# A two-block transformer on one core: GpSimd's elementwise work moved to VectorE, and the gate, up and MLP products turned feature-major

## The chip, the cores and the metric

The kernel runs on one core of a Trainium2 chip. TensorE multiplies, VectorE (DVE), ScalarE (ACT) and GpSimd (POOL) work element by element, SyncE (SP) issues the transfers of the weights. The metric is the time of one execution on the device in microseconds (us); less is better.

## The reference

The input is one sequence of 256 tokens with 1024 features, all in float32. Block 1 has two layers; a layer adds to the residual x a SwiGLU feed-forward (FFN), a mixer and a second FFN. Cut to the parts that the change touches:

```python
def ffn(x, w):                       # D = 1024, F = 2816
    h = rmsnorm(x) * w.norm
    x = x + 0.5 * (silu(h @ w.gate) * (h @ w.up)) @ w.down

def mixer(x, w):                     # one input projection w_in, one output projection w_out
    h = rmsnorm(x) * w.norm_mix
    # three branches: gated linear attention with per-channel decay (hg),
    # gated delta rule with short convolutions (q, k, v), gated linear recurrence (rg)
    x = x + concat(hg, delta, rg) @ w.out

def mlp(x, w):                       # in block 2
    h = rmsnorm(x) * w.g_pre_mlp
    x = x + rmsnorm(relu(h @ w.up) ** 2 @ w.down) * w.g_post_mlp     # 1024 -> 4096 -> 1024
```

Block 2 has one layer: retention and dilated attention with a gated sum (combine), the MLP above, and a gate with an additional input (PLE). All weight matrices are read once, 290 MB in all.

## The kernel before

Every weight comes in chunks of two 128-row tiles by 512 columns ([128, 2, 512], 512 KB), in the order of use, loaded by SP's queue into one of four `raw` buffers. A product is made in float32r, a reduced float32, and is exact by parts: the weight w is split into wh (rounded) and wl = w - wh, the operand x into xh and xl, and three products are accumulated: xh·wh, xh·wl, xl·wh. In `wchunk` ScalarE casts wh (line 94) and another engine subtracts wl: GpSimd (line 97) or VectorE (line 99). Which one, the text in `split_on` says, one letter a chunk in turn: "ppv" in the FFNs and in block 2, so two of three on GpSimd. In the mixer the letters stand behind each step's name in `MIX_ORDER`. There are three buffers each for wh and wl, so ScalarE's cast of a chunk waits until TensorE is through with the one three before.

There are two forms of product. `gemm_tok` (through `mm_tok`, lines 146 to 148) is token-major: the stationary operand is a tile of 128 tokens, the moving one 512 weight columns, the result [token, column]. `gemm_feat` (lines 190 to 192) is feature-major: the stationary operand is a tile of 128 weight columns, the moving one all 256 tokens, the result [column, token]. Both take the same chunks.

`ffn` goes over the hidden columns in groups of 512 (the last has 256). Gate g and up u come token-major; per tile of 128 tokens ScalarE makes tanh(r g / 2), where r is the norm's factor of a token, and VectorE (1 + tanh)·g (line 319) and the product with u and r²/2 (line 320). The down product needs the hidden values with columns on partitions, so `hidden_T` transposes them on TensorE, 128x128 at a time (line 295, tile htr), and `split` casts the high part (ScalarE, line 199) and subtracts the low part (VectorE, line 200). `mlp` does the same with a squared relu in place of the gate. `norm_T` transposes x, weights and splits it (ScalarE line 202, VectorE line 203; tiles xTh, xTl) and makes r; with `by_tok` it takes the first 128 tokens first (transposes of line 262), without it pairs of both token tiles (line 275).

The mixer's steps are written out in `MIX_ORDER`; besides remainders GpSimd takes some of its elementwise work: masks of the triangular solve (lines 718, 719), parts of the halving levels of the hg scores (lines 871, 900, 901, 903, by the letters of `HG_POOL`), and four operations of the recurrence (lines 988, 989, 995, 996). `r_broadcast` (lines 471, 472) puts r on all partitions along the token axis, by products with a matrix of ones; the mixer and block 2's entry use it. The framework's scheduler decides in which order the instructions of each engine are issued, from the order of the program and the free buffers; each engine then runs its own in that order.

Of the kernel before, what the change touches and what calls it, by code (L numbers as in the profile page):

```python
# [231 lines left out]
class Stream:  # L232
    """The residual stream, token-major, and its transposed and weighted form for the next product."""
# [67 lines left out]

def ffn(c, st, wT, wg, wu, wd, F):
    nc = c.nc
    xs, r = st.norm_T(wT)
    rh = c.small.tile([P, 2], F32, tag="rh", name=c.nm("rh"))
    rr = c.small.tile([P, 2], F32, tag="rr", name=c.nm("rr"))
    nc.vector.tensor_scalar(rh, r, 0.5, None, op0=ALU.mult)
    nc.vector.tensor_tensor(rr, rh, r, op=ALU.mult)
# [1204 lines left out]
```

## Time and profile before

| | before |
|---|---|
| median of 3 runs | 1861.69 us (1858.45 to 1861.82) |
| profiled execution, span from first to last instruction | 1858.6 us |
| TensorE (PE) busy | 1764.4 us, 95%, 9216 products |
| TensorE's weight loads (PEld) busy | 1488.6 us, 80% |
| VectorE (DVE) busy | 935.6 us, 50% |
| ScalarE (ACT) busy | 896.4 us, 48% |
| GpSimd (POOL) busy | 925.1 us, 50% |
| mean granted clock of TensorE | 0.974 |
| read from memory | 289.47 MB, 156 GB/s over the span |

The lowest of the runs (1858.45 us) is within 0.2 us of the span of the profiled execution, so little lies around the span. A busy share is a mean over the whole program: the FFNs, the mixers and block 2 differ. Products overlap, so the busy time of one is longer than the distance to the next; for what a product costs, the distance between starts is to be read.

### The profile page before, as it was taken

To read this page: it belongs to the slowest core of one execution; us is meant where nothing else is said; L and a number is where in the kernel's file an instruction comes from. 1 tells how busy PE (TensorE), PEld (TensorE's weight loads), DVE (VectorE), ACT (ScalarE), POOL (GpSimd) and SP (SyncE) were. 2 spreads that over 40 slices of the span, in tenths; PEclk is the share of its full clock that TensorE was granted. 3 is DMA by queue.
4 is the path that set the end of the run, shared out by engine and by line. 5 is a ranking of instruction groups with operands and counts; after the bars stand their busy time and mean duration, and the time that the engine had idled before them with its cause. 6 is when DMAs were issued, how large, how long until landed. Compare 5 with 4: busy or idle time off the path is not lost.

```text
span 1858.6 us, 24550 instructions
## 1 busy us (share of the span) xinstructions
PE 1764.4 (95%) x9216; PEld 1488.6 (80%) x9216; DVE 935.6 (50%) x1744; ACT 896.4 (48%) x1364; POOL 925.1 (50%) x449
## 2 busy tenths in 40 slices
PE   8999988999999999987889999999999999999995
PEld 6888877978888788877878888788878888778884
DVE  5334599853333332299964333533556543643246
ACT  4445563444444444455345445455444544555453
POOL 4556455235555555544415556454433455555561
PEclk9999988899999999998989999999999999999998
DMA  6546432235555555532224545455333456545561
GB/s 221 181 159 206 162 111 74 87 102 181 182 193 182 181 182 181 182 137 91 69 100 169 177 163 205 153 184 173 127 134 114 158 176 209 181 164 181 182 227 45
DMA packets 91639, 292.13 MB, mean 157 GB/s; under 512 B 11008, under 2 KB 23808, under 8 KB 91520
## 3 DMA queue, kind: packets, MB, share of 16 engines
q1 hardware_dynamic: 91376, 290.45, 46.0%
q8 instruction: 72, 1.18, 0.3%
q14 instruction: 47, 0.39, 0.1%
q10 hardware_dynamic: 144, 0.11, 0.0%
HBM read 289.47 MB, written 1.05 MB: 156 GB/s over the span
## 4 chain that ended last, share of the span: by engine, by line
PE 72%; DVE 15%; issue 6%; POOL 3%; ACT 2%; DMA 1%; DVEq 0%; SPq 0%; POOLq 0%; ACTq 0%
PE mm L147 21%; PE mm L148 21%; PE mm L146 20%; POOL wl L97 3%; DVE cv L628 2%; PE htr L295 2%; PE mm L191 1%; PE mm L192 1%; PE mm L190 1%; DVE scr L909 1%; DMA raw<-in_weights 1%; DVE wl L99 1%; ACT wh L94 1%; DVE hS L716 1%; DVE rxc L967 1%
## 5 line engine op out<-in xcount | busy, mean ns | idle before, releaser
L97 POOL TENSOR_TENSOR wl<-raw,wh 128x1024 fp32r<-128x1024 f32 (+2 forms) x359 | 839.1, 2340 | 808.3 <-ACT wh L94 754.4
L94 ACT CAST wh<-raw 128x1024 fp32r<-128x1024 f32 (+2 forms) x544 | 549.5, 1011 | 600.7 <-PE mm L148 442.6
L147 PE MATMUL mm<-wl,xTh 128*128 128x512 f32 (+2 forms) x1336 | 509.0, 383 | 10.1 <-DVE wl L99 8.8
L148 PE MATMUL mm<-wh,xTl 128*128 128x512 f32 (+2 forms) x1336 | 503.9, 381 | 8.3 <-DVE xTl L203 8.3
L99 DVE TENSOR_TENSOR wl<-raw,wh 128x1024 fp32r<-128x1024 f32 (+2 forms) x185 | 236.4, 1278 | 488.3 <-ACT wh L94 487.9
L146 PE MATMUL mm<-wh,xTh 128*128 128x512 f32 (+2 forms) x1336 | 474.1, 385 | 1.4 <-ACT wh L94 0.9
L147 PEld LDWEIGHTS mm<-wl,xTh 128*128 128x128 f32 x1336 | 254.5, 190 | 58.6 <-DVE wl L99 9.3
L148 PEld LDWEIGHTS mm<-wh,xTl 128*128 128x128 f32 x1336 | 253.4, 190 | 59.5 <-DVE xTl L203 11.2
L146 PEld LDWEIGHTS mm<-wh,xTh 128*128 128x128 f32 x1336 | 250.7, 190 | 51.8 <-ACT xTh L202 3.2
L147 PE MATMUL mm<-wl,hT 128*128 128x512 f32 x608 | 243.3, 401 | 2.8 <-POOL wl L97 2.6
L148 PE MATMUL mm<-wh,hT 128*128 128x512 f32 x608 | 240.3, 396 | 0.0
L146 PE MATMUL mm<-wh,hT 128*128 128x512 f32 x608 | 219.1, 397 | 4.8 <-DVE scr L571 4.8
L190 PE MATMUL mm<-xTh,wh 128*128 128x256 f32 x448 | 130.7, 295 | 14.1 <-DVE xp L620 14.1
L146 PEld LDWEIGHTS mm<-wh,hT 128*128 128x128 f32 x608 | 115.3, 190 | 30.8 <-DVE scr L571 5.2
L147 PEld LDWEIGHTS mm<-wl,hT 128*128 128x128 f32 x608 | 115.8, 190 | 29.6 <-POOL wl L97 5.4
L148 PEld LDWEIGHTS mm<-wh,hT 128*128 128x128 f32 x608 | 116.1, 191 | 24.4 <-DVE hT L203 0.3
L191 PE MATMUL mm<-xTl,wh 128*128 128x256 f32 x448 | 131.9, 296 | 1.1 <-DVE xTl L203 1.1
L192 PE MATMUL mm<-xTh,wl 128*128 128x256 f32 x448 | 129.6, 294 | 0.0
L190 PEld LDWEIGHTS mm<-xTh,wh 128*128 128x128 f32 x448 | 88.5, 198 | 15.8 <-issue 15.5
L191 PEld LDWEIGHTS mm<-xTl,wh 128*128 128x128 f32 x448 | 89.0, 199 | 3.4 <-DVE xTl L203 1.9
L192 PEld LDWEIGHTS mm<-xTh,wl 128*128 128x128 f32 x448 | 87.6, 198 | 2.0 <-issue 1.2
L200 DVE TENSOR_TENSOR hT<-htr,hT 128x512 fp32r<-128x512 f32 (+1 forms) x76 | 49.9, 660 | 75.6 <-ACT hT L199 75.6
(444 smaller groups left out, 1857.6 us busy)
## 6 DMA issues: line engine op xcount, KB each, us to landing
raw<-in_weights SPq DMA_DIRECT2D x514, 512.0 KB, 3.3
raw<-in_weights SPq DMA_DIRECT2D x32, 256.0 KB, 3.1
raw<-in_weights SPq DMA_DIRECT2D x16, 260.0 KB, 3.0
x_res<-in_x SPq DMA_DIRECT2D x2, 512.0 KB, 4.4
rowp<-in_b_gate SPq DMA_DIRECT2D x2, 512.0 KB, 5.3
out<-pg SPq DMA_DIRECT2D x4, 256.0 KB, 2.0
tab<-in_tab SPq DMA_DIRECT2D x1, 900.5 KB, 6.0
ctab<-in_tab SPq DMA_DIRECT2D x1, 900.0 KB, 9.5
```

Of the source, the lines that this page charges most:

```text
L94: nc.scalar.copy(h, raw)
L97: nc.gpsimd.tensor_tensor(l, raw, h.bitcast(F32), op=ALU.subtract)
L99: nc.vector.tensor_tensor(l, raw, h.bitcast(F32), op=ALU.subtract)
L146: nc.tensor.matmul(o, xh[:, kt, tok], wh[:, k], start=a and k == 0, stop=False)
L147: nc.tensor.matmul(o, xh[:, kt, tok], wl[:, k], start=False, stop=False)
L148: nc.tensor.matmul(o, xl[:, kt, tok], wh[:, k], start=False, stop=z and k == m - 1)
L190: nc.tensor.matmul(o, wh[:, k, cs], xh[:, kt], start=a, stop=False)
L191: nc.tensor.matmul(o, wh[:, k, cs], xl[:, kt], start=False, stop=False)
L192: nc.tensor.matmul(o, wl[:, k, cs], xh[:, kt], start=False, stop=z)
L200: nc.vector.tensor_tensor(l, src, h.bitcast(F32), op=ALU.subtract)
L295: nc.tensor.transpose(ps[:, b], hc[:, b * P:(b + 1) * P], c.ident)
L628: nc.vector.scalar_tensor_tensor(o[:, b], xp[:, b2, tap:tap + S], wc(tap), o[:, b], op0=ALU.mult, op1=ALU.add)
```

## The change

GpSimd does no elementwise operation with two inputs any more. All remainders wl are subtracted by VectorE (after the change in line 93), and the mixer's operations named above are VectorE's too; the letters in `MIX_ORDER` and `HG_POOL` go. GpSimd keeps fills, two kinds of copies and the identity: 44 instructions in place of 453.

In `ffn` gate and up are made with `gemm_feat`, and in `mlp` the up product. The results then already have columns on partitions, and 240 transposes of 128x128 go, in 56 sets of four and 8 sets of two. As r now lies along the free axis, `ffn` calls `r_broadcast`, VectorE multiplies the gate by it (line 321), and the residual addition takes over r/4. `norm_T` in `mlp` is called without `by_tok`.

```diff
 def wchunk(self, w, k0, nkt, c0, n, room=None):
         nc.scalar.copy(h, raw)
-        self.nw += 1
-        if self.split_on[self.nw % len(self.split_on)] == "p":
-            nc.gpsimd.tensor_tensor(l, raw, h.bitcast(F32), op=ALU.subtract)
-        else:
-            nc.vector.tensor_tensor(l, raw, h.bitcast(F32), op=ALU.subtract)
+        nc.vector.tensor_tensor(l, raw, h.bitcast(F32), op=ALU.subtract)
...
+def hidden_split(c, hT, hc, f0, nb):
+    k0 = f0 // P
+    h, l = hT[k0 // 8]
+    k0 %= 8
+    c.split(h[:, k0:k0 + nb], l[:, k0:k0 + nb], hc)
...
 def ffn(c, st, wT, wg, wu, wd, F):
     xs, r = st.norm_T(wT)
-    rh = c.small.tile([P, 2], F32, tag="rh", name=c.nm("rh"))
-    rr = c.small.tile([P, 2], F32, tag="rr", name=c.nm("rr"))
-    nc.vector.tensor_scalar(rh, r, 0.5, None, op0=ALU.mult)
-    nc.vector.tensor_tensor(rr, rh, r, op=ALU.mult)
+    rbc = r_broadcast(c, r)
+    rq = c.small.tile([P, 2], F32, tag="rr", name=c.nm("rr"))
+    nc.vector.tensor_scalar(rq, r, 0.25, None, op0=ALU.mult)
...
-        g = c.gemm_tok(xs, wg, 0, 8, c0, n)
-        u = c.gemm_tok(xs, wu, 0, 8, c0, n)
-        for t in range(2):
-            th = c.w2("th")[:, :n]
-            hc = c.w2("hc")[:, :n]
-            nc.scalar.activation(th, g[t][:, :n], AF.Tanh, scale=rh[:, t:t + 1])
-            nc.vector.scalar_tensor_tensor(th, th, 1.0, g[t][:, :n], op0=ALU.add, op1=ALU.mult)
-            nc.vector.scalar_tensor_tensor(hc, th, rr[:, t:t + 1], u[t][:, :n], op0=ALU.mult, op1=ALU.mult)
-            hidden_T(c, hT, hc, t, c0, n)
+        g = c.gemm_feat(xs, wg, 8, c0, n)
+        gs = []
+        for i in range(n // 256):
+            gn, th = v2(c.w2("gn"), 2), v2(c.w2("th"), 2)
+            nc.vector.tensor_tensor(gn, v2(g[i], 2), rb, op=ALU.mult)
+            nc.scalar.activation(th, gn, AF.Tanh, scale=0.5)
+            nc.vector.scalar_tensor_tensor(th, th, 1.0, gn, op0=ALU.add, op1=ALU.mult)
+            gs.append(th)
+        u = c.gemm_feat(xs, wu, 8, c0, n)
+        for i in range(n // 256):
+            nc.vector.tensor_tensor(gs[i], gs[i], v2(u[i], 2), op=ALU.mult)
+            hidden_split(c, hT, gs[i], c0 + 256 * i, 2)
...
-            nc.vector.scalar_tensor_tensor(xx, o[t], 0.5, xx, op0=ALU.mult, op1=ALU.add)
+            nc.vector.scalar_tensor_tensor(xx, o[t], rq[:, t:t + 1], xx, op0=ALU.mult, op1=ALU.add)
...
-MIX_ORDER = "rg:pvvp ba:pvvp k:pvpp gates dk solve0 hg:vppv vg:pppv hgs v:ppvp solve1 hgo both dv1 q:ppvp dv0 dq core0 core1 z:ppvv dout out:pvvvppvp".split()
+MIX_ORDER = "rg ba k gates dk solve0 hg vg hgs v solve1 hgo both dv1 q dv0 dq core0 core1 z dout out".split()
...
-            on = lambda i: nc.gpsimd if HG_POOL[i][lv] == "p" else nc.vector
-            on(0).tensor_tensor(Av[:, :, 1], cv[:, :, 1], ref, op=ALU.subtract)
+            nc.vector.tensor_tensor(Av[:, :, 1], cv[:, :, 1], ref, op=ALU.subtract)
...
 def mlp(self):
-        xs, r = st.norm_T(self.prm.col["g_pre_mlp_2"], by_tok=True)
+        xs, r = st.norm_T(self.prm.col["g_pre_mlp_2"])
...
-            u = c.gemm_tok(xs, self.a["w_up_2"], 0, 8, c0, 512)
-            for t in range(2):
-                hc = c.w2("hc")
-                nc.scalar.activation(hc, u[t], AF.Relu)
-                nc.vector.tensor_tensor(hc, hc, u[t], op=ALU.mult)
-                hidden_T(c, hT, hc, t, c0, 512)
+            u = c.gemm_feat(xs, self.a["w_up_2"], 8, c0, 512)
+            for i in range(2):
+                hc = v2(c.w2("hc"), 2)
+                nc.scalar.activation(hc, v2(u[i], 2), AF.Relu)
+                nc.vector.tensor_tensor(hc, hc, v2(u[i], 2), op=ALU.mult)
+                hidden_split(c, hT, hc, c0 + 256 * i, 2)
```

The order of the instructions moves at three places that matter here. The first is VectorE's queue in the first FFN, before; one group of 512 hidden columns stands here (th the gate, hc the hidden values, mm the results of products, htr the transposes of hc, hT the split hidden values, wl VectorE's third of the remainders):

```order
L99 TENSOR_TENSOR wl_439<-raw_436,wh_438 128x1024
L319 SCALAR_TENSOR_TENSOR th_490<-th_490,mm_342 128x512
L99 TENSOR_TENSOR wl_519<-raw_516,wh_518 128x1024
L320 SCALAR_TENSOR_TENSOR hc_491<-th_490,rr_161,mm_416 128x512
L319 SCALAR_TENSOR_TENSOR th_502<-th_502,mm_343 128x512
L320 SCALAR_TENSOR_TENSOR hc_503<-th_502,rr_161,mm_417 128x512
L200 TENSOR_TENSOR hT_165<-htr_495,hT_164 128x4x128
L99 TENSOR_TENSOR wl_573<-raw_570,wh_572 128x1024
L200 TENSOR_TENSOR hT_165<-htr_507,hT_164 128x4x128
```

and the same place after the change (gn the gate times r, rbcs the factor r on all partitions):

```order
L93 TENSOR_TENSOR wl_532<-raw_529,wh_531 128x1024
L93 TENSOR_TENSOR wl_574<-raw_571,wh_573 128x1024
L93 TENSOR_TENSOR wl_604<-raw_601,wh_603 128x1024
L321 TENSOR_TENSOR gn_559<-mm_437,rbcs_167 128x512
L321 TENSOR_TENSOR gn_564<-mm_438,rbcs_167 128x512
L93 TENSOR_TENSOR wl_634<-raw_631,wh_633 128x1024
L323 SCALAR_TENSOR_TENSOR th_560<-th_560,gn_559 128x512
L323 SCALAR_TENSOR_TENSOR th_565<-th_565,gn_564 128x512
L93 TENSOR_TENSOR wl_664<-raw_661,wh_663 128x1024
L93 TENSOR_TENSOR wl_702<-raw_699,wh_701 128x1024
L93 TENSOR_TENSOR wl_732<-raw_729,wh_731 128x1024
L327 TENSOR_TENSOR th_560<-th_560,mm_569 128x512
```

All eight remainders of a group now stand in the queue, two or three of them between the operations on the results; the splits (line 194) follow the next remainder.

The second place is the first mixer, VectorE's queue at the first halving levels of the hg scores (hA the exponents, hB keys, lines 900 to 903; sv and hS belong to the triangular solve that runs beside). Before:

```order
L900 TENSOR_TENSOR hA_2681<-scr_1797 128x4x64
L901 TENSOR_TENSOR hA_2681<-scr_1797 128x4x64
L877 COPY_PREDICATED hS_1795<-ident,hd_2660 128x1024
L909 TENSOR_TENSOR scr_1798<-hA_2681,scr_1797 64x4x64 x2
L900 TENSOR_TENSOR hA_2695<-scr_1797 128x8x32
L901 TENSOR_TENSOR hA_2695<-scr_1797 128x8x32
```

After:

```order
L93 TENSOR_TENSOR wl_3551<-raw_3548,wh_3550 128x1024
L904 TENSOR_TENSOR hB_3115<-hA_3114,scr_2230 128x512
L910 TENSOR_TENSOR scr_2231<-hA_3114,scr_2230 64x4x64 x2
L901 TENSOR_TENSOR hA_3128<-scr_2230 128x8x32
L902 TENSOR_TENSOR hA_3128<-scr_2230 128x8x32
L728 COPY_PREDICATED scr_2226<-ctab,sv_3363 128x512
L93 TENSOR_TENSOR wl_3581<-raw_3578,wh_3580 128x1024
L728 COPY_PREDICATED scr_2225<-ctab,sv_2771 128x512
L904 TENSOR_TENSOR hB_3129<-hA_3128,scr_2230 128x512
L910 TENSOR_TENSOR scr_2227<-hA_3128,scr_2230 64x4x64 x2
L901 TENSOR_TENSOR hA_3142<-scr_2230 128x16x16
```

The keys hB and the remainders wl, which GpSimd made, stand between VectorE's own steps.

The third place is VectorE's queue ahead of the PLE gate: the factor pr of token tile 1 after the MLP and the addition to the residual x_res. Before:

```order
L219 TENSOR_TENSOR rsa_15356<-rsa_15356,rsw_15355 128x1
L220 SCALAR_TENSOR_TENSOR rsy_15354<-rsa_15356,rsy_15354 128x1
L222 TENSOR_SCALAR rsw_15355<-rsy_15354 128x1
L223 SCALAR_TENSOR_TENSOR rsa_15356<-rsy_15354,rsw_15355,pm_2884_15348 128x1
L228 TENSOR_SCALAR rsy_15354<-rsy_15354,rr_13917 128x1
L229 SCALAR_TENSOR_TENSOR pr_2885_15349<-rsa_15356,rsy_15354 128x1
L1358 SCALAR_TENSOR_TENSOR x_res<-pf_15340,pr_2885_15349,x_res 128x512
L1358 SCALAR_TENSOR_TENSOR x_res<-pf_15344,pr_2885_15349,x_res 128x512
```

After:

```order
L214 SCALAR_TENSOR_TENSOR rsy_17374<-rsa_17376,rsy_17374 128x1
L93 TENSOR_TENSOR wl_17497<-raw_17494,wh_17496 128x1024
L216 TENSOR_SCALAR rsw_17375<-rsy_17374 128x1
L93 TENSOR_TENSOR hT_17517<-raw_17538,hT_17516 128x1024
L217 SCALAR_TENSOR_TENSOR rsa_17376<-rsy_17374,rsw_17375,pm_2816_17368 128x1
L197 SCALAR_TENSOR_TENSOR xTl_17389<-xtr_17391,colp,xTh_17388 128x128
L197 SCALAR_TENSOR_TENSOR xTl_17389<-xtr_17404,colp,xTh_17388 128x128
L222 TENSOR_SCALAR rsy_17374<-rsy_17374,rr_15633 128x1
L223 SCALAR_TENSOR_TENSOR pr_2817_17369<-rsa_17376,rsy_17374 128x1
L197 SCALAR_TENSOR_TENSOR xTl_17389<-xtr_17391,colp,xTh_17388 128x128
L1359 SCALAR_TENSOR_TENSOR x_res<-pf_17360,pr_2817_17369,x_res 128x512
L1359 SCALAR_TENSOR_TENSOR x_res<-pf_17364,pr_2817_17369,x_res 128x512
```

Two remainders (wl and hT, which is a wl in a borrowed buffer) and splits of tile 0's transposed residual (xTl) now stand within the chain.

## Rows read from the trace of the kernel before

**Rows 1.** Stretch, its us, busy us of PE, PEld, DVE, ACT, POOL; clock, DMA share, GB/s.

```profile
20.00:140.00 120.00, 120.00 (x580) 100.15 (x579) 41.07 (x47) 55.48 (x65) 65.82 (x30) 1.00 0.52 175
...
220.00:345.00 125.00, 104.49 (x726) 98.91 (x726) 118.02 (x196) 61.13 (x109) 61.10 (x44) 0.87 0.27 91
...
800.00:935.00 135.00, 111.27 (x841) 105.40 (x841) 127.98 (x226) 66.17 (x124) 62.68 (x46) 0.94 0.28 95
```

**Rows 2.** Groups by form, GpSimd, whole program: busy us, mean ns | idle before.

```profile
L97 POOL TENSOR_TENSOR wl<-raw,wh 128x1024 fp32r<-128x1024 f32 x331 | 802.9, 2428 | 745.8 <-ACT wh L94 691.9 <-issue 30.3 <-DVE rsw L217 7.0
```

**Rows 3.** Line 99: ns min/median/max, first and last start, forms.

```profile
L99 DVE TENSOR_TENSOR wl<-raw,wh x185: 687/1225/3324, 13.5 to 1799.0; 128x1024 fp32r<-128x1024 f32 x165, 128x512 fp32r<-128x512 f32 x12, 128x520 fp32r<-128x520 f32 x8
```

**Rows 4.** Timeline, VectorE, at the MLP's entry: start us, duration us, instruction.

```profile
1620.80 1.41 DVE L1358 SCALAR_TENSOR_TENSOR x_res<-pf,pr,x_res 128x512 f32<-128x512 f32 x2
```

**Rows 5.** Timeline, TensorE, in the first FFN around a set of transposes.

```profile
109.09 0.39 PE L146 MATMUL mm<-wh,xTh 128*128 128x512 f32 x1
...
109.33 0.60 PE L295 MATMUL htr<-ident,hc 128*128 128x128 f32 x4
...
110.00 0.39 PE L147 MATMUL mm<-wl,xTh 128*128 128x512 f32 x1
...
112.29 0.39 PE L148 MATMUL mm<-wh,xTl 128*128 128x512 f32 x1
```

**Rows 6.** Timeline, feature-major products in runs of 67 and 29, and a load.

```profile
232.23 0.28 PE L192 MATMUL mm<-xTh,wl 128*128 128x256 f32 x1
...
232.35 0.19 PEld L191 LDWEIGHTS mm<-xTl,wh 128*128 128x128 f32 x1
...
239.72 0.28 PE L192 MATMUL mm<-xTh,wl 128*128 128x256 f32 x1
...
1392.15 0.28 PE L191 MATMUL mm<-xTl,wh 128*128 128x256 f32 x1
...
1395.45 0.28 PE L192 MATMUL mm<-xTh,wl 128*128 128x256 f32 x1
```

**Rows 7.** Timeline, TensorE, r on all partitions in the first mixer.

```profile
216.78 0.61 PE L472 MATMUL rbc<-dg,ones 128*128 128x128 f32 x4
```

**Rows 8.** Timeline, GpSimd and VectorE at 262 to 266 us.

```profile
262.68 2.44 POOL L97 TENSOR_TENSOR wl<-raw,wh 128x1024 fp32r<-128x1024 f32 x1 [2.54 <-PE cumrow L602]
...
263.10 2.57 DVE L200 TENSOR_TENSOR hT<-rg,hT 128x512 fp32r<-128x512 f32 x1 [0.20 <-ACT hT L199]
```

**Rows 9.** Groups by form, VectorE, 220 to 345 us.

```profile
L628 DVE SCALAR_TENSOR_TENSOR cv<-xp,colp,cv 128x256 f32<-128x256 f32 x24 | 17.6, 776 | 0.0
...
L909 DVE TENSOR_TENSOR scr<-hA,scr 64x256 f32<-64x256 f32 x14 | 12.1, 863 | 0.1
...
L716 DVE COPY_PREDICATED hS<-ctab,LTm 32x128 f32<-32x128 int32 x8 | 9.0, 1125 | 0.1
...
L967 DVE SCALAR_TENSOR_TENSOR rxc<-rxp,colp,rxc 128x256 f32<-128x256 f32 x6 | 7.8, 1358 | 0.0
```

**Rows 10.** Lines 628, 909, 716: ns min/median/max, first and last start.

```profile
L628 DVE SCALAR_TENSOR_TENSOR cv<-xp,colp,cv x72: 431/473/2622, 248.4 to 940.9; 128x256 f32<-128x256 f32 x72
...
L909 DVE TENSOR_TENSOR scr<-hA,scr x28: 388/587/1811, 298.3 to 909.1; 64x256 f32<-64x256 f32 x28
...
L716 DVE COPY_PREDICATED hS<-ctab,LTm x16: 250/1033/2364, 275.4 to 869.7; 32x128 f32<-32x128 int32 x16
```

**Rows 11.** Timeline, VectorE and TensorE ahead of the PLE gate; idle in brackets.

```profile
1814.67 1.89 DVE L214 SCALAR_TENSOR_TENSOR rsw<-rsy,pm 128x1 f32<-128x1 f32 x1
...
1818.89 2.26 DVE L220 SCALAR_TENSOR_TENSOR rsy<-rsa,rsy 128x1 f32<-128x1 f32 x1
...
1822.97 0.45 PE L262 MATMUL xtr<-ident,x_res 128*128 128x128 f32 x1 [7.69 <-DVE x_res L1358]
```

**Rows 12.** Timeline, TensorE at the MLP's entry.

```profile
1616.07 1.29 PE L262 MATMUL xtr<-ident,x_res 128*128 128x128 f32 x8
```

**Rows 13.** Waits of GpSimd, 220 to 345 us: us in total, times, longest.

```profile
POOL wl L97 <- ACT wh L94: 36.5, 10, 6.0
```

More of the change, by code (lines that the diff above doesn't have):

```diff
@@ L70, in __init__ @@
         self.n = 0
-        self.nw = 0
         self.nx = 0
         self.xtags = ("xa", "xb")
-        self.split_on = "ppv"
         nc = self.nc
@@ L304, in ffn @@
     xs, r = st.norm_T(wT)
[L305 to L308 removed]
+    rbc = r_broadcast(c, r)
+    rq = c.small.tile([P, 2], F32, tag="rr", name=c.nm("rr"))
+    nc.vector.tensor_scalar(rq, r, 0.25, None, op0=ALU.mult)
     KF = F // P
     hT = [c.hT_tile(j) for j in range((KF + 7) // 8)]
+    rb = bc(rbc.unsqueeze(1), [P, 2, S])
     for c0 in range(0, F, 512):
         n = min(512, F - c0)
[L313 to L321 removed]
+        g = c.gemm_feat(xs, wg, 8, c0, n)
[10 more added lines that the diff above has]
+            hidden_split(c, hT, gs[i], c0 + 256 * i, 2)
     for c0 in (0, 512):
@@ L479, in v2 @@
     return ap.rearrange("p (a b) -> p a b", a=a)
-MIX_ORDER = "rg:pvvp ba:pvvp k:pvpp gates dk solve0 hg:vppv vg:pppv hgs v:ppvp solve1 hgo both dv1 q:ppvp dv0 dq core0 core1 z:ppvv dout out:pvvvppvp".split()
-HG_POOL = ("vvvppvp", "ppvppvv")
+MIX_ORDER = "rg ba k gates dk solve0 hg vg hgs v solve1 hgo both dv1 q dv0 dq core0 core1 z dout out".split()
 class Mixer:
@@ L534, in __init__ @@
         for s in MIX_ORDER:
-            s, _, on = s.partition(":")
-            c.nw, c.split_on = -1, on or "pv"
             steps[s]()
@@ L539, in __init__ @@
                 c.xtags = ("xb",)
-        c.nw, c.split_on = -1, "ppv"
     def project(self, w_out):
@@ L717, in delta_solve @@
         nc.vector.transpose(f(Tc), f(TTc))
-        nc.gpsimd.tensor_tensor(LT32, LT, h4(K["mt32"]), op=ALU.mult)
-        nc.gpsimd.tensor_tensor(LT, LT, h4(K["mt64"]), op=ALU.mult)
+        nc.vector.tensor_tensor(LT32, LT, h4(K["mt32"]), op=ALU.mult)
+        nc.vector.tensor_tensor(LT, LT, h4(K["mt64"]), op=ALU.mult)
         for b in (2, 4, 8, 16):
@@ L870, in hg_scores @@
         qk = v2(c.w2("hqk"), 2)
-        nc.gpsimd.tensor_tensor(qk, q, k, op=ALU.mult)
+        nc.vector.tensor_tensor(qk, q, k, op=ALU.mult)
         pd = c.x_tile("hd")
@@ L898, in hg_scores @@
             ref = bc(cv[:, :, 0, b - 1:b], [P, 4 * n, b])
-            on = lambda i: nc.gpsimd if HG_POOL[i][lv] == "p" else nc.vector
-            on(0).tensor_tensor(Av[:, :, 1], cv[:, :, 1], ref, op=ALU.subtract)
-            on(0).tensor_tensor(Av[:, :, 0], ref, cv[:, :, 0], op=ALU.subtract)
+            nc.vector.tensor_tensor(Av[:, :, 1], cv[:, :, 1], ref, op=ALU.subtract)
+            nc.vector.tensor_tensor(Av[:, :, 0], ref, cv[:, :, 0], op=ALU.subtract)
             nc.scalar.activation(A, A, AF.Exp)
-            on(1).tensor_tensor(B, A, k, op=ALU.mult)
+            nc.vector.tensor_tensor(B, A, k, op=ALU.mult)
             g = lambda a: a.rearrange("p j (t n two b) -> p (j t) n two b", t=2, two=2, b=b)
@@ L987, in rg @@
         nc.scalar.activation(m, m, AF.Sqrt, scale=-1.0)
-        nc.gpsimd.tensor_scalar(ti, ti, 1.0, 0.5, op0=ALU.add, op1=ALU.mult)
-        nc.gpsimd.tensor_tensor(ti, ti, xc, op=ALU.mult)
+        nc.vector.tensor_scalar(ti, ti, 1.0, 0.5, op0=ALU.add, op1=ALU.mult)
+        nc.vector.tensor_tensor(ti, ti, xc, op=ALU.mult)
         nc.vector.tensor_tensor(m, m, ti, op=ALU.mult)
@@ L994, in rg @@
         nc.scalar.activation(g2, gx, AF.Square)
-        nc.gpsimd.tensor_scalar(g2, g2, 0.044715, 1.0, op0=ALU.mult, op1=ALU.add)
-        nc.gpsimd.tensor_tensor(g2, g2, gx, op=ALU.mult)
+        nc.vector.tensor_scalar(g2, g2, 0.044715, 1.0, op0=ALU.mult, op1=ALU.add)
+        nc.vector.tensor_tensor(g2, g2, gx, op=ALU.mult)
         nc.scalar.activation(g2, g2, AF.Tanh, scale=0.7978845608028654)
```

## The prediction

> **What bounds the kernel now.** I read the table of stretches first, then the groups by form, and then the timeline at the places where TensorE stops. In the first feed-forward layer TensorE is busy the whole time, 120.00 of 120 us at 20 to 140 and at full clock, while VectorE is busy for a third [rows 1]; the other three and the MLP look the same. There only what TensorE itself executes counts. In the two mixers it is the reverse: at 220 to 345 and 800 to 935 TensorE is busy 104.49 of 125 and 111.27 of 135 us at clock 0.87 and 0.94, and VectorE 118.02 and 127.98, nearly without a pause [rows 1]. So the change has to be costed twice: by TensorE's own instructions in the FFNs and the MLP, by VectorE's load in the mixers. Beyond these there are a few places where a chain of small VectorE operations holds TensorE.
>
> **The remainders (wl) in the FFNs and the MLP.** One remainder of 128x1024 takes GpSimd 2428 ns [rows 2] and VectorE 1225 ns in the median [rows 3]. A group of 512 hidden columns has 8 weight chunks of 12 wide products each; at the pitch below (0.229 us) that is 96 x 0.229 = 22.0 us of TensorE. VectorE gets in the same time 8 x 1.225 = 9.8 us of remainders and eight operations of 128x512: the scaling by r, the gate, the product with u and the split, each twice. At 0.70 us each (the residual addition, 1.41 us for two [rows 4]) that is 5.6 us, in all 15.4 of 22.0, or 70%. The order shows two remainders ahead of each operation that waits for a finished product, which is 5.5 us of TensorE's work in hand. I cost the move at 0 here; the cover is TensorE's 22.0 us, and if VectorE were late at each of the 28 groups of the four FFNs and the MLP (5 full ones per FFN, 8 in the MLP, whose groups are half as long) by one operation of 0.7 us it would be +20.
>
> **Transposes.** 240 go: 56 sets of four and 8 sets of two. Around one set the wide products start at 109.09 and, with the four transposes and one other product between, at 110.00: 0.91 us for two steps. From 110.00 to 112.29 there are ten steps, 0.229 each [rows 5]. So a set of four costs 0.91 - 0.46 = 0.45 us, and a set of two about 0.22: 56 x 0.45 + 8 x 0.22 = 27 us. TensorE has no pause in these stretches, so the whole of it is on the path: **-27**.
>
> **Feature-major products.** 2304 products of 512 columns become 4608 of 256. The kernel has that form already in the mixers and in block 2. From 232.23 to 239.72 there are 66 steps, 0.1135 each; from 1392.15 to 1395.45 there are 28, 0.1179 each [rows 6]. Against 2304 x 0.229 = 528 us that is 523 by the first (-5) and 543 by the second (+15). Most runs of this form that I looked at lie at the first; I take 0, and keep -5 and +15 for the range.
> Each of these products loads its own weights, and a load lasts 0.19 us [rows 6], more than the pitch. Were loads to stand in the open, the 2304 additional ones would be 2304 x 0.19 = +438. The rows exclude that for this form: a pitch of 0.1135 is shorter than one load, so loads run beside products.
> The Trainium skill's page "TensorE: Matmul & The Clock Gate", section "What overlaps and what doesn't" under row and column tiling (Part 3), says that a weight load overlaps running matmuls only when its row group differs, and all loads here use the full 128 rows. By that page's load time (128 columns / 1.2, about 107 ns; an estimate from the page) the doubled loads would be about +247 us. The trace does not agree: products with full-height loads follow one another at 0.1135 us.
>
> **r on all partitions.** Each FFN now makes r as a row (two fp32 products with ones, and a copy). The mixer's one takes TensorE 0.61 us [rows 7]; four are **+2**, 0 to +2.4. It is needed only by the evacuation of the first gate group, some 11 us of products after the start.
>
> **The mixers.** At 220 to 345 GpSimd is busy 61.10 us, at 800 to 935 62.68 [rows 1]. All but some 2 us of fills goes to VectorE, at 1225 / 2428 of the time: +30 per mixer. What VectorE gets back is the time in which its operations stand still beside GpSimd's: at 263.10 a split of 0.7 us lasts 2.57 while a GpSimd remainder of 262.68 runs for 2.44 [rows 8]. By groups, mean in the stretch less the shortest of the same line [rows 9, 10]: convolution taps 24 x (776 - 431) = 8.3 us; keys of the halving levels 14 x (863 - 388) = 6.7; masked copies of the solve 8 x (1125 - 250) = 7.0; RG-LRU taps, which have the shape and operation of L628, 6 x (1358 - 431) = 5.6; the split 1.9. Sum 29.5, and smaller groups add a few us. So VectorE's load is about level: I take -2 a mixer, **-4** in all. Ends: if the standing still was not due to GpSimd, +30 a mixer; if VectorE gets 35 back and the mixer's chain of steps shortens with it (a step that GpSimd does in 2.43 us takes 1.2), -15 a mixer.
>
> **Entries.** Before the PLE gate TensorE waits 7.69 us for the residual [rows 11]. The chain of one-column operations there contains three that last about 2 us each (1.89 and 2.26 are shown, the third lies between them) where its other steps take about 0.2, each beside a GpSimd remainder. They give back 5.6 us; the order puts two remainders (2.45) and three splits of 128x128 (about 0.3 each) into the chain: **-2**. Before the MLP the transposes of token tile 0 now wait for tile 1's residual. They start at 1616.07 in the trace of before [rows 12]; tile 1's residual addition begins at 1620.80 [rows 4], and about 2 us earlier when the eight splits of tile 0 no longer stand in its chain. TensorE would pause for some 4 us there, of which it loses a part now too, since its first products come singly between the splits of tile 0; I take half: **+2**, 0 to +4.
>
> **Sum.** -27 + 0 + 2 - 4 - 2 + 2 = -29 on a span of 1858.6 us, that is 1830. The profiled execution's span lies 3 us under the median of the runs shown (1861.69) and at the lowest of them; I forecast the runs' median in the middle, **1831**.
>
> **Rivals.**
> *A, the mixers gain more.* The contention falls and the serial steps shorten: 15 us a mixer in place of 2, so 1831 - 26 = **1805**. For it: VectorE is the engine that is never free there, and its slowest operations are those beside GpSimd. Against it: GpSimd's work lay beside VectorE's and now lies in its queue. Chance 0.2.
> *B, VectorE stalls in the mixers where GpSimd waited.* GpSimd's remainders wait 36.5 us for ScalarE's casts in the first mixer's stretch, in 10 waits of up to 6.0 [rows 13], and nobody stands behind them. On VectorE's queue the solve and the levels stand behind such a wait, and TensorE behind these. If half is paid, 18 a mixer, the time is 1831 + 40 = 1871; if all, about 1908. It turns the sign from 15 us a mixer. For it: the order puts remainders between the solve's masked copies. Against: VectorE's own remainders hardly wait there now, since casts run ahead while VectorE is behind. Chance 0.12, at **1875**.
> *C, the narrow products run at the slower pitch.* +15: **1846**. One of the two runs shown speaks for it, and the FFN streams 512 KB chunks as that place does. Chance 0.12. With loads in the open (the +438 above) the time would be about 2270; chance 0.01.
> *D, the GpSimd half changes nothing measurable at the mixers and entries*: 1831 + 4 = 1835, inside the forecast's own range.
>
> **Numbers.** The forecast (1820 to 1842) has 0.55, A 0.2, B 0.12, C 0.12, open loads 0.01. The range 1803 to 1855 holds the forecast, C and most of A, and leaves B out. A measurement of this kernel tells about 0.2% (4 us) from no change. Slower: B's larger part and open loads, 0.11; the same: 0.03; faster: the rest, 0.86.
>
> **What would show it.** FFN stretches with TensorE busy throughout, each FFN shorter by 4 to 5 us, the MLP by about 7; narrow products 0.1135 apart there; no transposes of hc; VectorE at some 70%. In the mixers the taps at about 430 ns, no operation of 2.5 us, VectorE still busy nine tenths, and stretches within 5 us of before. A chain before the PLE gate of some 6 us. Wrong would be: waits of VectorE for ScalarE's casts in the mixers (B), mixers shorter by over 10 us each (A), a narrow pitch of 0.118 (C), or TensorE waiting for wl in the FFNs.

## The result, and the profile after

The changed kernel takes 1797.99 us in the median (1796.44 to 1802.76, 4 runs), the kernel before 1861.2 (1858.45 to 1861.82, 4 runs); the ratio is 0.9665 (0.9652 to 0.9678). That is 63 us less, where 30 were forecast, and below the range.

The page of the profiled execution after, busy time of each engine, its share of the span and its instructions:

```profile
PE 1734.5 (97%) x11296; PEld 1568.8 (87%) x11296; DVE 1207.1 (67%) x2181; ACT 892.3 (50%) x1352; POOL 13.4 (1%) x40
```

GpSimd is down from 925.1 to 13.4 us, VectorE up from 935.6 to 1207.1. That is 272 us more, though the 359 remainders of line 97 alone are 331 x 1.225 + 28 x 0.7 = 425 us of VectorE's time: what it did before takes less time now. Five lines of it, durations in ns (min/median/max) over the whole program; the first three answer to [rows 10], the fourth to the last of [rows 9], the fifth to [rows 3]:

```profile
L630 DVE SCALAR_TENSOR_TENSOR cv<-xp,colp,cv x72: 431/479/500, 241.1 to 905.5; 128x256 f32<-128x256 f32 x72
...
L910 DVE TENSOR_TENSOR scr<-hA,scr x28: 402/418/423, 290.3 to 872.7; 64x256 f32<-64x256 f32 x28
...
L718 DVE COPY_PREDICATED hS<-ctab,LTm x16: 283/297/307, 268.9 to 831.2; 32x128 f32<-32x128 int32 x16
...
L968 DVE SCALAR_TENSOR_TENSOR rxc<-rxp,colp,rxc x12: 475/478/480, 218.3 to 782.8; 128x256 f32<-128x256 f32 x12
...
L93 DVE TENSOR_TENSOR wl<-raw,wh x544: 676/1225/1227, 9.4 to 1756.1; 128x1024 fp32r<-128x1024 f32 x168, 128x512 fp32r<-128x512 f32 x10, 128x520 fp32r<-128x520 f32 x4
```

The maxima of 2622, 1811, 2364 and 3324 ns are gone; no operation of these lines stands still any more.

Both mixers whole, from the last down product of the FFN before to the last output product; columns as in [rows 1]. Before:

```profile
205.60:407.40 201.80, 176.25 (x1205) 163.97 (x1204) 168.51 (x320) 98.35 (x183) 81.03 (x60) 0.90 0.28 94
...
787.20:990.50 203.30, 172.66 (x1206) 159.17 (x1205) 168.47 (x322) 97.94 (x185) 79.64 (x56) 0.92 0.30 100
```

After:

```profile
202.90:385.60 182.70, 168.08 (x1199) 158.79 (x1198) 155.55 (x359) 97.98 (x179) 5.54 (x17) 0.93 0.32 102
...
763.60:945.50 181.90, 166.38 (x1200) 156.57 (x1199) 156.45 (x361) 97.52 (x180) 3.46 (x13) 0.93 0.35 111
```

The first mixer is 19.1 us shorter, the second 21.4. VectorE's busy time fell by 13.0 and 12.0, although GpSimd's 80 us went to it; the rest is time in which VectorE paused. TensorE's granted clock, as a mean over the stretch (1.00 is its level of 2.4 GHz, 0.50 that of 1.2), rose from 0.90 to 0.93 in the first, from 0.92 to 0.93 in the second.

To see where the time went, I divided each trace at the start of TensorE's last weight product of each phase (the columns of the weight products add up to the same 3306240 in each kernel, so the borders are at the same place of the program). Times in us; the four kernels on the right belong to the experiments:

```
                     before    after  feat_only  dve_only  mix_dve   reset5
FFN 1.1 gate and up  132.93   130.10     128.54    127.70   132.85   125.27
FFN 1.1 down          63.26    63.43      66.57     61.82    63.19    64.02
mixer 1              201.81   182.77     201.42    183.06   179.79   184.27
FFN 1.2 gate and up  126.63   129.03     126.91    128.39   128.91   125.00
FFN 1.2 down          62.21    61.25      62.00     61.66    62.16    61.96
FFN 2.1 gate and up  128.55   125.62     127.38    126.51   128.53   121.52
FFN 2.1 down          62.37    62.06      61.75     61.69    62.17    61.30
mixer 2              203.26   181.85     202.37    185.45   178.49   191.23
FFN 2.2 gate and up  126.93   129.21     126.92    128.71   128.99   124.82
FFN 2.2 down          62.50    61.93      62.07     61.92    62.69    61.22
block 2 to combine   435.74   427.88     436.17    427.94   437.26   427.75
MLP                  192.06   184.34     185.85    189.10   192.05   184.17
PLE                   39.87    33.98      41.77     33.92    40.18    35.42
```

Before against after: the mixers -40.4, block 2 up to combine -7.9, the MLP -7.7, PLE -5.9, and the four FFNs together only -2.8.

The narrow products are not alike everywhere. TensorE's timeline after, in the first FFN (20 steps between these rows) and in the MLP (19 steps); start us, duration:

```profile
59.81 0.28 PE L185 MATMUL mm<-xTl,wh 128*128 128x256 f32 x1
...
62.17 0.28 PE L184 MATMUL mm<-xTh,wh 128*128 128x256 f32 x1
...
1599.77 0.28 PE L186 MATMUL mm<-xTh,wl 128*128 128x256 f32 x1
...
1601.92 0.28 PE L184 MATMUL mm<-xTh,wh 128*128 128x256 f32 x1
```

That is 0.118 in the FFN and 0.113 in the MLP: the two values of [rows 6].

At the entries, VectorE ahead of the PLE gate and TensorE there and at the MLP's entry; idle time in brackets:

```profile
1755.20 0.16 DVE L214 SCALAR_TENSOR_TENSOR rsy<-rsa,rsy 128x1 f32<-128x1 f32 x1
...
1756.12 1.22 DVE L93 TENSOR_TENSOR wl<-raw,wh 128x1024 fp32r<-128x1024 f32 x1 [0.77 <-ACT wh L92]
...
1758.33 0.51 PE L140 MATMUL mm<-wh,xTh 128*128 128x512 f32 x1 [2.48 <-ACT xTh L196]
...
1569.26 2.82 PE L269 MATMUL xtr<-ident,x_res 128*128 128x128 f32 x12 [3.48 <-DVE x_res L1359]
```

The one-column operation of 2.26 us in [rows 11] takes 0.16; the longest wait at the PLE gate is 2.48 us in place of 7.69, since TensorE now goes on with tile 0's products ahead of the residual of tile 1. The MLP's entry has the pause that was forecast, 3.48 us. Block 2's entry had the same trouble as the PLE gate, unseen by me: the weighting of the residual there, before and after,

```profile
L1109 DVE TENSOR_TENSOR xw<-x_res,rowp x4: 679/2032/2901, 1148.8 to 1181.6; 128x512 f32<-128x512 f32 x4
```

```profile
L1110 DVE TENSOR_TENSOR xw<-x_res,rowp x4: 682/684/686, 1106.5 to 1139.6; 128x512 f32<-128x512 f32 x4
```

went from 2032 to 684 ns in the median of four. That GpSimd was the cause at these two entries is read from such durations; the runs below with unread GpSimd work have it in the mixers only.

### The profile page after: what moved, and what is told of

Read it like the earlier page. It is cut to its first block, busy times and chain, and to the rows that moved or that the text cites. A ratio compares the mean times of both kernels' runs of the same rounds, so it can differ in the third digit from the quotient of the medians.

```text
span 1794.7 us, 28677 instructions
## 1 busy us (share of the span) xinstructions
PE 1734.5 (97%) x11296; PEld 1568.8 (87%) x11296; DVE 1207.1 (67%) x2181; ACT 892.3 (50%) x1352; POOL 13.4 (1%) x40
## 4 chain that ended last, share of the span: by engine, by line
PE 90%; DVE 6%; ACT 2%; issue 1%; DMA 1%; SPq 0%; DVEq 0%; ACTq 0%
PE mm L185 13%; PE mm L186 13%; PE mm L184 13%; PE mm L140 13%; PE mm L141 13%; PE mm L142 13%; PE sv L711 2%; DVE wl L93 1%; ACT wh L92 1%; PE pv L1234 1%; PE dS L658 1%; PE dsc L1202 1%; PE hS L915 1%; PE dsc L1201 0%; DVE cv L630 0%
## 5 line engine op out<-in xcount | busy, mean ns | idle before, releaser
L93 DVE TENSOR_TENSOR wl<-raw,wh 128x1024 fp32r<-128x1024 f32 (+2 forms) x544 | 639.8, 1177 | 462.8 <-ACT wh L92 461.4
L184 PE MATMUL mm<-xTh,wh 128*128 128x256 f32 x2112 | 595.6, 284 | 13.1 <-DVE xp L622 10.0
L185 PE MATMUL mm<-xTl,wh 128*128 128x256 f32 x2112 | 598.0, 284 | 2.2 <-DVE xTl L197 2.1
L186 PE MATMUL mm<-xTh,wl 128*128 128x256 f32 x2112 | 595.2, 283 | 0.8 <-DVE wl L93 0.7
L184 PEld LDWEIGHTS mm<-xTh,wh 128*128 128x128 f32 x2112 | 401.4, 191 | 17.9 <-ACT th L572 10.4
L185 PEld LDWEIGHTS mm<-xTl,wh 128*128 128x128 f32 x2112 | 402.5, 191 | 4.7 <-DVE xTl L197 3.7
L186 PEld LDWEIGHTS mm<-xTh,wl 128*128 128x128 f32 x2112 | 403.0, 191 | 2.8 <-DVE wl L93 1.3
L141 PE MATMUL mm<-wl,xTh 128*128 128x512 f32 (+1 forms) x440 | 169.3, 386 | 0.0
L142 PEld LDWEIGHTS mm<-wh,xTl 128*128 128x128 f32 x440 | 83.0, 189 | 16.6 <-issue 2.0
L141 PEld LDWEIGHTS mm<-wl,xTh 128*128 128x128 f32 x440 | 82.9, 188 | 16.2 <-issue 1.9
```

Of the source, the lines that this page charges most:

```text
L141: nc.tensor.matmul(o, xh[:, kt, tok], wl[:, k], start=False, stop=False)
L142: nc.tensor.matmul(o, xl[:, kt, tok], wh[:, k], start=False, stop=z and k == m - 1)
L184: nc.tensor.matmul(o, wh[:, k, cs], xh[:, kt], start=a, stop=False)
L185: nc.tensor.matmul(o, wh[:, k, cs], xl[:, kt], start=False, stop=False)
L186: nc.tensor.matmul(o, wl[:, k, cs], xh[:, kt], start=False, stop=z)
```

## The experiments

The theories were: (1) VectorE stands still beside GpSimd's operations, and that is what the mixers and entries gained; (2) remainders and keys come sooner when VectorE makes them; and, for the FFNs, (P) the two fp32 products of `r_broadcast` leave the stream of narrow products in the slower of two steady spacings.

### One half each, and the mixers alone

`feat_only` is the kernel before with `ffn`, `hidden_split` and `mlp` of after; `dve_only` is after with `ffn` and `mlp` of before; `mix_dve` is before with only the mixers' share moved:

```diff
-MIX_ORDER = "rg:pvvp ba:pvvp k:pvpp gates dk solve0 hg:vppv ..."
+MIX_ORDER = "rg:v ba:v k:v gates dk solve0 hg:v ..."
-HG_POOL = ("vvvppvp", "ppvppvv")
+HG_POOL = ("vvvvvvv", "vvvvvvv")
-        nc.gpsimd.tensor_tensor(LT32, LT, h4(K["mt32"]), op=ALU.mult)
+        nc.vector.tensor_tensor(LT32, LT, h4(K["mt32"]), op=ALU.mult)
...
```

> The feature-major half alone; GpSimd keeps its remainders and its work in the mixers. If the two halves are independent: transposes -27, r on all partitions +2, and the narrow products at 0.1178 in the four FFNs (4224 of 256 columns, against half as many of 512 at 0.229: +14) and at 0.1133 in the MLP (-1): 12 us less than before, near 1849, with the mixers as before (about 202 us each from the end of the FFN's down product to the end of the output projection). Rival: VectorE's remainders are what lets the feature-major FFN run, so that GpSimd's slower ones stop TensorE in the FFNs and this is no faster than before (1861 or more).

Measured: 1851.96 us against 1861.46, ratio 0.9955 (0.9939 to 0.9972), 9.5 less, where 12 were forecast. The table has the MLP 6.2 shorter, the FFNs 3.2 together, the mixers within 1 us of before.

> The GpSimd half alone; FFN and MLP token-major with transposes as before. Theory 1 (VectorE stood still beside GpSimd, in the mixers and at the entries of block 2 and the PLE gate): the mixers gain 18 us each, the entries 12 together, so 48 less than before, near 1813. Rival (the recorded sum: VectorE's load level, -4 in the mixers and -2 at the entries): near 1855, and then the two halves need each other.

Measured: 1799.67 us, 0.9671 (0.9657 to 0.9686), 61.8 less. Nearly the whole gain is in this half; 48 were forecast. The mixers give 36.6 of it, block 2's and PLE's entries 13.8, the FFNs 7.0 and the MLP 3.0. The halves do not add up: 9.5 and 61.8 make 71, the whole change gained 63. On top of this half the feature-major one is worth 1.7 us (1799.67 to 1797.99), less than the 4 us that can be told from none.

> Before with only the two mixers' GpSimd work on VectorE; FFNs and block 2 keep two of three remainders on GpSimd, products are token-major. Theory 1: the mixers' 18 us each and nothing at the entries: near 1825. If the gain comes from the entries or from remainders outside the mixers: above 1850.

Measured: 1822.22 us, 0.9797 (0.9771 to 0.9822), 39.2 less; the mixers are 22.0 and 24.8 shorter (more than in `dve_only`; why is not shown), the gate and up products behind each 2 longer, and all else is within 1.6 us of before.

### Contention by itself

In `junk_sub` VectorE does all its work as after, in the same order; GpSimd subtracts as well, for nothing, in the mixers and of the chunks that it had before:

```diff
         nc.vector.tensor_tensor(l, raw, h.bitcast(F32), op=ALU.subtract)
+        self.nw += 1
+        if self.junk_on[self.nw % len(self.junk_on)] == "p":
+            for k in range(nkt):
+                for c1 in range(0, n - 255, 256):
+                    x, y = raw[:, k, c1:c1 + 256], h[:, k, c1:c1 + 256].bitcast(F32)
+                    nc.gpsimd.tensor_tensor(self.junk, x, y, op=ALU.subtract)
```

> After, and in the mixers GpSimd also subtracts raw - wh of those chunks that it had before, in pieces of 256 columns into a tile that nobody reads; VectorE does all its own work as after, and nobody waits for GpSimd's results. Theory 1 (contention): operations of VectorE of 2 to 2.6 us come back and the mixers grow by 20 to 30 us each, so 1838 to 1858. Rival theory 2 (the mixers gained because remainders and keys come 1.2 us sooner in the chain, and GpSimd's presence costs nothing): within 5 us of after, 1798 to 1803.

Measured: 1848.44 us (ratio to before 0.9929, 0.9912 to 0.9946), 50 more than after's 1797.99. The mixers, columns as above, and below them two lines of VectorE (the RG-LRU taps and the convolution taps) and GpSimd's unread subtractions, ns min/median/max:

```profile
203.30:409.30 206.00, 180.51 (x1200) 168.61 (x1199) 182.42 (x360) 97.98 (x179) 94.29 (x100) 0.88 0.28 90
...
791.20:996.30 205.10, 177.15 (x1199) 164.49 (x1198) 184.87 (x362) 97.08 (x180) 92.18 (x96) 0.88 0.30 98
```

```profile
L979 DVE SCALAR_TENSOR_TENSOR rxc<-rxp,colp,rxc x12: 943/954/961, 219.3 to 814.4; 128x256 f32<-128x256 f32 x12
...
L641 DVE SCALAR_TENSOR_TENSOR cv<-xp,colp,cv x72: 438/477/955, 250.4 to 958.4; 128x256 f32<-128x256 f32 x72
...
L101 POOL TENSOR_TENSOR junk<-raw,wh x176: 724/802/5154, 199.4 to 998.2; 128x256 f32<-128x256 f32 x176
```

VectorE is busy 27 and 28 us longer than after, at the same work; the RG-LRU taps take 954 ns in place of 478. The operations of 2 to 2.6 us that were expected did not come back: GpSimd's pieces are shorter here than the remainders were (a median of 802 ns against 2.4 us), and only some of the convolution taps lay beside one (median 477 as after, longest 955). The mixers are 23.3 and 23.2 longer, the gate and up products behind each 4, and the clock is 0.88. Theory 2 is out as the main cause: nobody reads what GpSimd makes here. It does hold the buffers of its chunks, but ScalarE's cast waited for it only once a mixer, for 2.2 and 1.3 us.

`junk_copy` is the same with `nc.gpsimd.tensor_copy(self.junk, x)`, one input in place of two.

> As the run before with GpSimd's unread work, but copies of the same pieces of raw (one input) in place of subtractions (two inputs). If any GpSimd traffic makes VectorE stand still: mixers 20 us longer or more each, as with the subtractions, less in the ratio of GpSimd's busy time. If only GpSimd's operations with two inputs do it: within 5 us of after, near 1798 to 1803.

Measured: 1802.77 us (0.9681, 0.9666 to 0.9696), 4.8 more than after's 1797.99. The mixers:

```profile
203.00:389.20 186.20, 167.51 (x1200) 157.32 (x1199) 161.79 (x360) 97.71 (x179) 52.94 (x99) 0.93 0.31 100
...
767.80:952.10 184.30, 166.00 (x1200) 155.73 (x1200) 162.84 (x362) 98.04 (x180) 54.56 (x95) 0.94 0.35 109
...
L101 POOL COPY junk<-raw x176: 391/418/1492, 192.3 to 925.9; 128x256 f32<-128x256 f32 x176
```

GpSimd is busy 53 and 55 us there, and VectorE 6 longer than after; by the table the mixers are 3.4 and 2.4 longer. The same pieces subtracted gave GpSimd 89 us a mixer beyond its work in after, copied 47 and 51; so a microsecond of subtracting cost VectorE 0.30 us and one of copying 0.13, and in the ratio of GpSimd's time the copies would have made the mixers 12 us longer. Copies cost less, but not nothing. Each is also shorter, and that bears on it: over the whole traces, an operation of VectorE beside one of these copies lasted at most 0.24 us longer than the same one usually does in after, beside one of the subtractions at most 0.59, and beside a remainder of 128x1024 (2.5 us in `wl_pool` below) up to 2.25, so never longer than the GpSimd operation itself. Whether the second input counts beyond the length is not separated here.

### The remainders against the rest

`wl_pool` is after, with the mixers' remainders divided by the letters of before; masks, keys and exponents stay on VectorE.

```diff
-        nc.vector.tensor_tensor(l, raw, h.bitcast(F32), op=ALU.subtract)
+        self.nw += 1
+        on = nc.gpsimd if self.split_on[self.nw % len(self.split_on)] == "p" else nc.vector
+        on.tensor_tensor(l, raw, h.bitcast(F32), op=ALU.subtract)
```

> After, with the mixers' remainders divided between GpSimd and VectorE as before; the other elementwise work stays on VectorE. By contention each us of GpSimd's two-input work costs VectorE about as much as it takes off: GpSimd gets some 40 us a mixer of remainders, VectorE is relieved of 20 and stands still for 25 to 35: 5 to 15 us a mixer longer, 1808 to 1828. If moving the remainders made no difference and the masks, keys and exponents did: within 5 us of 1798.

Measured: 1838.24 us, against 1796.65 of after on the same chip; 41.6 more, where 10 to 30 were forecast (ratio to before 0.9877, 0.9853 to 0.9901). In the profiled execution (1842.94) the mixers are 29.0 and 23.7 longer than after, the gate and up products behind them 7 and 3 shorter. The mixers, and GpSimd's remainders by form:

```profile
203.40:415.10 211.70, 189.11 (x1206) 175.57 (x1205) 170.91 (x337) 98.14 (x181) 59.20 (x40) 0.85 0.27 89
...
785.90:991.50 205.60, 179.32 (x1206) 166.39 (x1205) 171.63 (x339) 97.75 (x182) 56.90 (x36) 0.90 0.30 99
...
L96 POOL TENSOR_TENSOR wl<-raw,wh 128x1024 fp32r<-128x1024 f32 x40 | 100.9, 2524 | 725.5 <-ACT wh L93 718.5 <-DVE rsw L214 7.0
...
L96 POOL TENSOR_TENSOR wl<-raw,wh 128x520 fp32r<-128x520 f32 x8 | 11.0, 1376 | 40.6 <-ACT wh L93 40.6
```

VectorE is rid of 20 large and 4 small remainders a mixer, 20 x 1.225 + 4 x 0.69 = 27 us, and is yet busy 15 us longer than after: some 42 us of standing still for the 56 us that GpSimd's remainders take a mixer, 0.75 per microsecond. GpSimd's help with the remainders costs VectorE more than it saves.

### The two spacings

`mlp_rbc` adds a call of `r_broadcast` to `mlp`, its result unread.

> After, with an additional r on all partitions in the MLP, whose result nobody reads. Theory P (the two fp32 products of it leave the stream of narrow products in the slower of two steady spacings, 0.1178, as in the FFNs; the MLP has none and runs at 0.1133): most of the MLP's 768 narrow products go to 0.1178, +3 us, and the products themselves +0.6. Rival (the spacing hangs on the operands or weights of the FFN): the MLP stays at 0.1133, +0.6 us.

Measured: 1799.43 us; the MLP's up product 99.90 against 95.81. TensorE's timeline around it:

```profile
1576.96 0.28 PE L184 MATMUL mm<-xTh,wh 128*128 128x256 f32 x1
...
1578.32 0.28 PE L184 MATMUL mm<-xTh,wh 128*128 128x256 f32 x1
...
1578.44 0.61 PE L479 MATMUL rbc<-dg,ones 128*128 128x128 f32 x4
...
1579.01 0.28 PE L186 MATMUL mm<-xTh,wl 128*128 128x256 f32 x1
...
1579.95 0.28 PE L185 MATMUL mm<-xTl,wh 128*128 128x256 f32 x1
```

12 steps ahead of the fp32 products are 0.113 each, 8 steps behind them 0.1175, and so to the end of the MLP (+4.1, forecast 3.6).

One case may be chance, so I looked at every call of `r_broadcast` in a feature-major FFN or MLP, in all kernels without the transposes below: 33 calls in eight kernels. Behind 31 the stream runs at 0.1178 to its end. Where at least 20 steps of the stream stand ahead of the call to tell, it was at 0.113 to 0.114 ahead of 17, and all 17 changed to the slower spacing; it was at 0.1178 ahead of 5, and 4 stayed there. In after itself only the second and third FFN show the change: in the first and the last the stream is at the slower spacing already ahead of r's products. The two calls with the faster spacing behind them are the first FFN of `feat_only` and the second of `wl_pool`, and in both the slower one stood ahead (6 and 52 steps).

`ffn_reset`, and `reset5`, the same kernel again with more rounds, put two transposes behind them, `all_reset` does it in the mixers and block 2's entry as well:

```diff
-def r_broadcast(c, r):
+def r_broadcast(c, r, extra=0):
...
+    for i in range(extra):
+        nc.tensor.transpose(ps[:, S + i * P:S + (i + 1) * P], dg, c.ident)
...
-    rbc = r_broadcast(c, r)
+    rbc = r_broadcast(c, r, 2)
```

> After, with two transposes of 128x128, whose result nobody reads, right behind the two fp32 products in each FFN. Theory P, with the addition that transposes bring the stream back (after the transposes of the norm it was seen at 0.1133): the 1056 narrow products of each FFN run at 0.1133, 4.7 us less each, with 0.2 us for the transposes: 18 us less, near 1780. If what follows the fp32 products doesn't matter, or the spacing hangs on something else: the FFNs stay at 0.1178 and the time rises by about 1 us, near 1799.

> The changed kernel itself, timed beside the three below for a closer comparison: 1798, as before.

> The kernel with two transposes behind r's products in each FFN, again. Its FFNs each took 4 us less, but the median was only 3 us below that of the changed kernel, with a mixer 10 us longer at a lower clock. If that clock was chance of the run: 1782 to 1788. If it stays lower in the second mixer whenever the FFN ahead is shorter: 1792 to 1796.

> The two transposes behind r's products everywhere, so in the mixers and at block 2's entry too. Theory P: the mixers' feature-major products are at 0.1178 in their undisturbed runs only, some 400 of about 960 a mixer, so 1 to 2 us a mixer less than with the FFNs alone; VectorE's load hides part of it: 0 to 4 us less in all.

Measured: `ffn_reset` 1794.95 us (0.9648, 0.9624 to 0.9671); on another chip `after5` 1796.65 (0.9652, 0.9628 to 0.9676), `reset5` 1791.72 (0.9623, 0.9602 to 0.9643), `all_reset` 1787.61 (0.9605, 0.9581 to 0.9629). The 1780 forecast for `ffn_reset` did not come. `all_reset` lies 4 us below `reset5`, with intervals that overlap. The first FFN in `reset5`, 21 steps between the rows:

```profile
59.81 0.28 PE L185 MATMUL mm<-xTl,wh 128*128 128x256 f32 x1
...
62.19 0.28 PE L185 MATMUL mm<-xTl,wh 128*128 128x256 f32 x1
```

0.113: gate and up are 4.0 to 4.8 us shorter in all four FFNs. Of these 17 us the kernel keeps 5. The second mixer's input products, from the end of the FFN ahead, give most of the rest back; after and in `reset5`, to about the same product:

```profile
763.60:885.00 121.40, 115.68 (x928) 112.45 (x927) 113.70 (x256) 71.06 (x125) 2.81 (x10) 0.99 0.38 120
```

```profile
752.80:884.00 131.20, 124.71 (x932) 121.12 (x930) 118.22 (x271) 71.80 (x127) 2.41 (x9) 0.92 0.37 119
```

Measured to one and the same product it is 121.6 after and 130.9 in `reset5`, 9.3 us longer at a clock of 0.92 against 0.99. The other two kernels with the transposes take 131.8 (`ffn_reset`, 0.91) and 132.3 (`all_reset`, 0.96). Without the transposes it is 122.5 in `after5` (0.97), but 133.2 in `ffn_twice` (below, 0.95), so the clock is not the whole of it. Why this stretch is longer and its clock lower in one kernel and not in another I have not settled.

`ffn_twice` has two further fp32 products with the ones in place of the transposes.

> After, with two further fp32 products with the ones behind r's products in each FFN, where the reset had two transposes; their result isn't read. If it is the transposes that bring the stream back to the faster spacing: the FFNs stay at 0.1178 and gate and up take what they took after the change (130, 129, 126, 129 us) and 0.6 us more. If any further instructions there do it (a shift of the stream by some steps): 0.1133 in most of the FFNs and 4 us less in each, as with the transposes.

Measured: 1806.5 us in one run; gate and up 130.10, 129.48, 126.07 and 129.65 us, so as after plus 0.4 or nothing: two more fp32 products do not bring the faster spacing back, two transposes do.

## Why the prediction was wrong, by its own steps

**VectorE's load in the mixers, "about level", is the step that failed.** -4 was forecast for both mixers, -40 came, and with the mixers' GpSimd work alone moved 47 (`mix_dve`); the FFN behind each mixer gave back 2. The mechanism was the one named: operations standing still beside GpSimd's. The size was not. I summed four groups and one split to 29.5 us in the first mixer's busiest 125 us. Those came back nearly as worked out: over the whole first mixer their durations add up to 27 us less (the convolution taps from a mean of 677 ns to 477). What I left aside, "a few us", was not small: by the sum of durations, all that VectorE does there in both kernels takes 46 us less, so 18 lie outside what I had summed. The work that it took over costs it 38 in the whole mixer, where I had set 30 from those 125 us. The steps of the logarithm on eight columns, for one of the rest, in the trace of before, in ns,

```profile
L383 DVE TENSOR_TENSOR la<-la,lz x18: 154/166/2350, 6.9 to 820.1; 128x8 f32<-128x8 f32 x12, 128x4 f32<-128x4 f32 x6
```

reach 2350 for an operation of 166, 2.2 us in the first mixer; a one-input step of 128x2 (rsa<-rsw) took 2418 there and takes 163 after. Rows of that kind stand all over the chain, and their excess does not show among the costliest groups. VectorE's busy time in the whole mixer fell by 12 to 13 us where I had -2 (it counts overlapping ends once, which sums of durations do not), and its pauses by 6 to 9 on top. Rival A had the direction, its 15 a mixer were still too little. The end of my bounds on the other side (+30) assumed that the standing still was not GpSimd's doing; `junk_sub` shows that it was.

**Rival B did not occur.** VectorE's waits for ScalarE's casts in the mixers did not grow into a stall: they are 9.2 and 11.6 us, none above 2.8, where they were 11.9 and 16.2, up to 9.8. Rival D's time does not follow from the sum: without the -4 and the -2 it is 1837, not 1835.

**The transposes** were right, **the narrow products at 0** were not. FFN 2.1, which has another FFN ahead of it, shows both: on top of `dve_only` its gate and up take 0.89 us less, where its transposes (-4.94), r's products (+0.61) and 1056 products at 0.1178 in place of 528 at 0.229 (+3.48) make -0.85. The MLP runs at the faster spacing; there the same step is worth 4.8 us on top of `dve_only`, with 7.2 for its 16 sets of transposes, 0.9 for the products and its entry's pause of 3.48 us against it. In the four FFNs nearly all of the 4224 products ran at 0.118, which is rival C: 4224 x 0.1178 - 2112 x 0.229 = 14 us where I had 0, most of what the FFNs' transposes were worth (4 x 4.9). On top of `dve_only` the feature-major FFNs cost 4.2 us in all, where these terms make -3. The rest lies in places that I had not priced: at the program's start the products reach their full pace at 18.0 us, in `dve_only` at 14.0; ahead of the first down product there is a wait of 1.91 for a remainder; and the two FFNs behind mixers are some 1.5 us each above these terms, which stays open. I had the two spacings in the rows, and gave C 0.12, since I took the faster one for the usual one; I had not asked what the stream had met just before it.

**Remainders in the FFNs at 0**: nearly right in its own terms (after, TensorE waited for wl twice in the four FFNs, 1.9 and 0.5 us), but beside it the FFNs won 7 us with VectorE's half alone. Most of that lies in the first one (6.7), and there at the program's start: the products reach their full pace at 21.7 us before and at 14.0 in `dve_only`.

**The entries**: -2 for PLE was -5.9, 0 for block 2 was -7.9; both were undersized in the way of the mixers (operations beside GpSimd's that I had not summed), as far as durations show. The MLP's entry came within its 0 to 4: the step's 4.8 us leave it 3.3, where I took 2.

The errors partly cancelled: 36 us too little from the mixers, 12 from the entries and 2.5 from the MLP, 15 too much from the FFNs.

The rule on weight loads that the prediction set against the rows (the Trainium skill, "TensorE: Matmul & The Clock Gate", "What overlaps and what doesn't") is not borne out: the gate, up and MLP products of 256 columns, each with a load of the full 128 rows, start 0.113 or 0.118 apart. Another page bears on the mixers: the Trainium skill's "GPSIMD Engine Reference", section "Key points", says that GpSimd shares its SBUF interfaces with VectorE and that the contention is with VectorE's instructions in a two-port mode or with two SBUF inputs. The runs agree for the taps (two SBUF inputs, 954 against 478 ns), and add that it matters what GpSimd does: the same pieces copied cost VectorE 6 us a mixer, subtracted 27. Operations with one input stood still too (rsa<-rsw, 2418 against 163 ns); whether they ran in a two-port mode no trace shows.

## What to carry to other kernels

An engine that shares a path with the bottleneck engine is not free help: ask how long the bottleneck's own operations last beside it, over all its operations and the smallest above all, not over the costliest groups. Work that looks divided can be cheaper undivided; a run in which the helper works for nobody shows that there is a price. Its size hangs on the helper's operations: 0.30 us per microsecond in pieces of 256 columns here, 0.75 in the kernel's own remainders. And a price per instruction that takes two values in a trace is a condition to be looked for, not a scatter to be averaged.

## What the runs showed of the hardware that I had not expected

A GpSimd subtraction of 128x1024 (2.4 us) makes VectorE stand still for most of it, so that 56 us of such work cost VectorE 42. Subtractions of 128x256 cost it 27 for 89 us, copies of the same pieces 6 for 47. The stream of float32r products of 256 columns has two steady spacings, 0.1133 and 0.1178 us, each of which lasts for hundreds of products; two fp32 products with a matrix of ones within the stream were followed by the slower one in 31 of 33 calls, two transposes behind them by the faster one in all four FFNs of `ffn_reset`, `reset5` and `all_reset`. It does not hang on these alone: the MLP's up product takes 99.02 us in `junk_copy` and 100.55 in `wl_pool`, at the slower one, with neither in it, and `feat_only`'s first FFN and `wl_pool`'s second run at the faster one behind r's products. What sets it stays open.
